# Four edits around the second layer of a two-layer trunk: first weight sections asked for earlier, the z weights split on other engines, one pair without squares, a later row split

## The chip, the cores and the metric

One core of one Trainium2 chip runs the whole kernel. The metric is the device time of one execution in microseconds, as the median of several runs; a profiled execution gives the trace. Engines are called PE (TensorE), DVE (VectorE), ACT (ScalarE), POOL (GpSimd) and SP (SyncE, whose queue issues the transfers).

## The reference

Two layers over x (1024 tokens, 1024 channels), each x <- x + W_out(mixer(RMSNorm(x)) * silu(z)), with z from the same input projection as the mixer's operands; a final RMSNorm follows.

```python
def fox_mixer(h, w_in, b_f, w_out):            # layer 0
    q, k, v, f, z = split(h @ w_in)
    ...                                        # causal attention with a forget gate, 16 heads of 64
    return (o * silu(z)) @ w_out

def nsa_mixer(h, w_in, pe_k, w_ck1, w_ck2, pe_v, w_cv1, w_cv2, w_out):   # layer 1
    q, kc_raw, vc_raw, ks_raw, vs_raw, kw_raw, vw_raw, gate_raw, z = split(h @ w_in)
    kc = compress_blocks(kc_raw, pe_k, w_ck1, w_ck2)
    vc = compress_blocks(vc_raw, pe_v, w_cv1, w_cv2)
    ...                                        # compressed, selected and window attention, three gates
    return (o * silu(z)) @ w_out

def compress_blocks(x, pe, w1, w2):
    ...
    return silu(blk @ w1) @ w2
```

## The kernel before, in words

Every product is taken with operands split into a high and a low part: `mm3` (L224 to L227) issues three matmuls, high by high (L225), high by low (L226), low by high (L227). Layer 0 holds the parts in a 32-bit format, the input projections of layer 1 in F16. An F16 weight is scaled by a power of two first; that scale comes from sums of squares of the weights, which `early.step` gathers during layer 0: each call clears a bias (L181), squares one 128x512 piece on ACT (L182) and then asks for the next piece on SP (L172), with one buffer, so that a piece is asked for when the square before it is done. Calls stand in the K, V, Q and Z sections of the pairs of heads; the V section is `fox_v` (L495), with its two calls at L509, for every pair but pair 0.

**The boundary of the layers.** `out_rest0` (L795) makes the last eight token tiles' results of layer 0 in the order 4, 5, 6, 7, 3, 0, 1, 2: the y matmuls, an add on DVE (L825), squares on ACT, the norm on DVE (L103 to L109, result h_n), then `after0`, which stores the row (L846) and calls `to_hT`: eight transposes on PE (L119, tile pth_n), the high part on ACT (L123), the low part on DVE (L124), into hT, whose half 0 holds tiles 0 to 3 and half 1 tiles 4 to 7. After that `scales`, `section` and `next_w` start layer 1: `next_w` keeps two weight sections ahead, by `load_w16` (L137 to L141, the load of wst) and `split_w16` (L146): high part in one DVE instruction (L147), low part either on DVE in two (L156) or, for kc, v, ka, kr and z, on POOL in eight, four that scale in place (L151) and four that subtract (L152). The first section takes the keys kc0 and kc1 together: half 1 with kc0, half 1 with kc1, then half 0 with each.

**The z weights.** While layer 1's projections and compression run, `load_z` (L901 to L919) brings and splits one of eight z sections at a time: a bias on ACT (zr, L911), then `split_w16` on DVE and POOL, then the next load on SP (zst, L918, one buffer). Nothing uses zw before 970 us. The compression's first product for vc (`cmp_mlp`, hid_vc) takes per step l a load of w_vc (L999), a cast w1h on DVE (L1002), a difference w1l on POOL (L1003), and bh on ACT (L1007) and bl on DVE (L1008), with two buffers for w1h and w1l; between its steps stand sections of q (pn_qr).

**The row split at the end.** `out_start` of layer 1 waits until the first rows of the gated output are stored, loads them (of, L1424), and after `yield 2000` splits them: ohi on ACT (L1429), olo on DVE (L1430). A yield's number is the time that the program gives to other strands of the interleaved code before it takes this one up again. All orders are fixed when the program is built: each engine runs its own list in order.

Of the kernel before, what the change touches and what calls it, by code (L numbers as in the profile page):

```python
# [8 lines left out]
F32 = mybir.dt.float32  # L9
# [4 lines left out]
AF = mybir.ActivationFunctionType  # L14
OP = mybir.AluOpType
# [21 lines left out]
def f(ap):  # L37
    return ap.bitcast(F32)
# [3 lines left out]
def tile_fox_nsa(ctx, tc, a, out):  # L42
# [94 lines left out]
    def load_w16(staged, src, name, scale, gp=False):  # L137


        st = staged.tile([P, KC, P], F32, tag="wst", bufs=1, name=f"wst_{name}")  # L140
        dma(st, src)  # L141
        parts = [wp.tile([P, KC, P], F16, tag=f"w{x}", bufs=2, name=f"w{x}_{name}") for x in ("hi", "lo")]
        return split_w16(st, scale, parts, gp)

    def split_w16(st, scale, parts, gp):
        hi, lo = parts  # L146
        V.tensor_scalar(hi, st, scale, None, OP.mult)  # L147
        if gp:
# [347 lines left out]
    def fox_v(p):  # L496

        w = next_w()
        v = sa.tile([P, 2, 2, 4, P], F16, tag="v", bufs=2, name=f"v_{p}")
        sc = sa.tile([P, 4], F32, tag="vsc", bufs=3, name=f"vsc_{p}")  # L500
        vT = []
        for half in range(2):
            pt = ps_a(f"v{p}_{half}")
            yield from project(w, hT, half, pt)
            vT.append(f(sa.tile([P, 512], F32R, tag="Q", bufs=8, name=f"vT_{p}_{half}")))
            A.activation(vT[half], pt, AF.Abs, accum_out=sc[:, half:half + 1])
            A.copy(vT[half], pt)
            if p:
                early.step(vT[half][:, 0:1])  # L509
        channel_scale(sc, 2, 1 / UP)  # L510
        for half in range(2):
            vs = sa.tile([P, 2, 512], F16, tag="vs", bufs=2, name=f"vs_{p}_{half}")
            A.activation(vs[:, 0], vT[half], AF.Copy, scale=sc[:, 3:4])
            V.scalar_tensor_tensor(vs[:, 1], vT[half], sc[:, 3:4], vs[:, 0], OP.mult, OP.subtract)
            nc.sync.dma_start_transpose(v[:, half].rearrange("p c t d -> p (c t) d"), vs.rearrange("p c t -> p (c t)"))
        ready["v", p] = v, sc[:, 2:3]
# [275 lines left out]
    cols2 = [slice(half * 512, half * 512 + 512) for half in range(2)]  # L792
    gain = []

    def out_rest0(ow, w, after):  # L795

        gB = ow.tile([P, D], F32, name="gB0")
        dma(gB, a["norm_g"][1:2, :].to_broadcast([P, D]))
        gain.extend(gain_scale(gB))
        lh, ll = (ow.tile([P, D], F32R, name=f"o7{x}") for x in "hl")  # L800
        for half in (1, 0):
            dma(f(ll[:, cols2[half]]), oF[7 * P:8 * P, cols2[half]])
        xs0[3] = sk.tile([P, D], F32, tag="KL", name="xr0_3")
        dma(xs0[3], a["x"][3 * P:4 * P, :])
        of, oh, ol = out_tiles("0_3")
        dma(of[:, 0:7, :], oF[0:7 * P, 3 * P:4 * P].rearrange("(k p) t -> p k t", p=P))
        for half in (1, 0):
            A.copy(lh[:, cols2[half]], f(ll[:, cols2[half]]))
            V.tensor_tensor(ll[:, cols2[half]], f(ll[:, cols2[half]]), f(lh[:, cols2[half]]), OP.subtract)
        pend = []  # L810
        for t in (4, 5, 6, 7, 3, 0, 1, 2):
            tk = slice(t * P, (t + 1) * P)
            if t == 3:
                A.copy(oh[:, 0:7, :], of[:, 0:7, :])
                V.tensor_tensor(ol[:, 0:7, :], of[:, 0:7, :], f(oh[:, 0:7, :]), OP.subtract)
# [12 lines left out]
            if len(pend) > 2:
                after(*pend.pop(0))
        for x in pend:  # L830
            after(*x)
# [10 lines left out]
    hT = [[x[:, i] for i in range(2)] for x in hT]  # L842
    ow = tc.alloc_tile_pool(name="ow", bufs=1, reuse_waits="tile")

    def after0(t, xt, h):
        dma(x1[t * P:(t + 1) * P, :], xt)  # L846
        to_hT(h, t, hT, f"n1_{t}")

    out_rest0(ow, ready["wout"], after0)
    W, E = {}, {}  # L850

    def scales(r, kinds, name):


        V.tensor_scalar(r[:, 2], r[:, 1], 2.0 ** 77, None, OP.mult)
        V.tensor_scalar(r[:, 3], r[:, 0], gain[0], 2.0 ** 50, OP.mult, OP.mult)
        for i, x in enumerate(kinds):
            W[x], E[x] = r[:, 2, i:i + 1], r[:, 3, i:i + 1]

    def bound(n, e, sign, name):  # L860

# [5 lines left out]
        return u[:, 0:1], u[:, 1:2]  # L867

    r1 = first[0]
    scales(r1, ("kc", "vc", "q", "z", "g"), "early")  # L870
    rq, eq = bound(r1[:, 1, 2:3], E["q"], -1.0, "q")
    ow.release()
    sk.release()
# [16 lines left out]
    oD = dram.tile([8, 2, P, 512], F32, name="oD")  # L890

    pers = tc.alloc_tile_pool(name="pers", bufs=1, side="right")
    gates = pers.tile([P, NT, 48], F32, name="gates")
    selb = pers.tile([P, GR, 4, 16], F32, name="selb")
    vinv = pers.tile([P, GR], F32, name="vinv")
    pa = tc.alloc_tile_pool(name="pa", bufs=1, reuse_waits="tile")

    nsa_w = [("kc", 0), ("kc", 1), ("qa", 0), ("qa", 1), ("vc", 0), ("vc", 1)]
    nsa_w[4:4] = [("qr", i) for i in range(2)]
    kvo = [("v", 0), ("v", 2), ("v", 1), ("v", 3), ("ka", 0)] + [("kr", i) for i in range(3)]  # L900
    nsa_w += [("qr", i) for i in range(2, 6)] + kvo  # L901
    zt = [h1.tile([P, 4, 2, KC, P], F16, tag=f"h{x}1", name=f"zw{x}") for x in (1, 0)]
    zw = [[zt[p // 4][:, p % 4, x] for x in range(2)] for p in range(8)]

    def load_z(x=None):


        if zload:
            p, st = zload.pop()
            r = pa.tile([P, 1], F32, tag="zr", bufs=2, name=f"zr_{p}")  # L910
            A.activation(r, x, AF.Identity, bias=W["z"], scale=0.0)  # L911
            split_w16(st, r, zw[p], True)
            p += 1
        else:
            p = 0
        if p < 8:
            st = pa.tile([P, KC, P], F32, tag="zst", bufs=1, name=f"zst_{p}")
            dma(st, a["nsa_w"][20 + p])  # L918
            zload.append((p, st))  # L919

    nsa_i = {"kc": 0, "vc": 2, "qa": 4, "qr": 6, "ka": 12, "kr": 13, "v": 16, "z": 20}
    nq, wq = list(nsa_w), []

    def next_w(key):
        while len(wq) < 2 and nq:
            kind, i = nq.pop(0)
            wq.append(((kind, i), load_w16(pers if len(nq) % 2 else wp, a["nsa_w"][nsa_i[kind] + i], f"n{kind}{i}",
                                           W[kind if kind in W else kind[0]], kind in ("kc", "v", "ka", "kr"))))
        k, w = wq.pop(0)
        assert k == key  # L930
        return w

    def section(keys, use):

# [14 lines left out]

    def late_scales():  # L950
        r = roots(sums[:, 41:49], ((0, 4), (4, 8)), "late", pers)
        scales(r, "kv", "late")
        rk, ek = bound(r[:, 1, 0:1], E["k"], 1.0, "k")
        u = pers.tile([P, 4], F32, name="units")
        inverse(u[:, 0:1], rq, rk, SCALE)
        V.tensor_scalar(u[:, 1:2], u[:, 0:1], -1.0, None, OP.mult)
        V.tensor_scalar(u[:, 2:3], E["z"], 0.5, None, OP.mult)
        V.tensor_tensor(u[:, 3:4], E["z"], E["v"], OP.mult)
        ready["units"] = [u[:, i:i + 1] for i in range(4)]
        ready["ek"] = ek  # L960
# [213 lines left out]
    gst = pa.tile([P, KC, 48], F32, name="gst")  # L1174
    dma(gst, a["nsa_w_g"].rearrange("(k p) c -> p k c", p=P))
    gw = pa.tile([P, KC, P], F16, tag="vt", bufs=1, name="gw")
    G.tensor_copy(gw, zero[:, :, None].to_broadcast([P, KC, P]))
    V.tensor_scalar(gw[:, :, 0:48], gst, W["g"], None, OP.mult)
    V.scalar_tensor_tensor(gw[:, :, 64:112], gst, W["g"], gw[:, :, 0:48], OP.mult, OP.subtract)

# [220 lines left out]
    def out_start(rows1):  # L1401
# [29 lines left out]

        yield lambda: met(0)
        load(0)
        yield 2000
        split(0)
        for n, (t, k0, stop) in enumerate(parts):
            if n == 2:
# [338 lines left out]
```

## Time and profile before

| | us |
|---|---|
| median of 3 runs | 1483.13 |
| lowest, highest | 1483.09, 1487.86 |
| profiled execution, its own time | 1481.62 |
| its span | 1479.8 |
| busy PE, DVE, ACT, POOL | 1380.7, 1094.8, 872.1, 600.1 |

The span is the time from the first to the last instruction of the profiled execution. Busy shares are means over stages with different limits, so the places of the edits are read each in its own stretch: its waits on PE, the granted clock there (1.00 is full speed), and the instructions of the other engines in order of time.

### The profile page before, as it was taken

What the parts mean: (1) busy time and instruction counts of PE and PEld (TensorE: products, weight loads), DVE (VectorE), ACT (ScalarE), POOL (GpSimd) and SP (SyncE); (2) the same over time, 40 slices, a digit from 0 to 9 for tenths busy, and PEclk for the clock granted to TensorE, in tenths of its full rate; (3) what the DMA queues carried; (4) which work ended last, traced back from release to release, by engine and by line L of the source; (5) the groups of instructions that cost most, each with busy time, mean ns of one, the idle gap of its engine ahead of it and who ended that gap; (6) DMA issues with size and microseconds to landing.
All of it is one profiled execution on the core that took longest, in us unless ns stands there. A gap on an engine that the chain in (4) does not pass through costs nothing. (4 is left out here: it accounts for less than half of the span.)

```text
span 1479.8 us, 30155 instructions
## 1 busy us (share of the span) xinstructions
PE 1380.7 (93%) x10491; PEld 998.3 (67%) x10491; DVE 1094.8 (74%) x2874; ACT 872.1 (59%) x2190; POOL 600.1 (41%) x816
## 2 busy tenths in 40 slices
PE   5999999999999898989998898889999989999998
PEld 4877888888888767854544444447666766766776
DVE  6586677787877778676754475978988878889844
ACT  5376667676654655345422176657777768787523
POOL 2232323333232320031334665435766657687400
PEclk9999999999999999989998999999999999999999
DMA  7887798988877898454443346646577676677434
GB/s 250 265 177 178 186 196 191 210 180 202 166 162 154 198 214 182 142 172 144 129 125 105 108 128 153 143 128 113 126 153 160 138 165 128 135 157 156 104 136 148
DMA packets 413513, 237.01 MB, mean 160 GB/s; under 512 B 334448, under 2 KB 373040, under 8 KB 413104
## 3 DMA queue, kind: packets, MB, share of 16 engines
q1 hardware_dynamic: 413360, 235.07, 65.9%
q8 instruction: 83, 1.36, 0.4%
q14 instruction: 70, 0.57, 0.1%
HBM read 121.55 MB, written 37.81 MB: 108 GB/s over the span
## 5 line engine op out<-in xcount | busy, mean ns | idle before, releaser
L1532 PE MATMUL S_n<-nk,nq 128*128 128x320 f16 (+5 forms) x768 | 153.3, 314 | 10.1 <-DVE m_n L1540 7.5
L718 ACT ACTIVATE P<-P,m 128x512 f32<-128x512 f32 (+1 forms) x192 | 116.5, 608 | 77.3 <-DVE m L709 76.7
L689 POOL TENSOR_TENSOR Bd<-B,tri 128x128 f32<-128x128 f32 x128 | 62.2, 501 | 240.0 <-DVE m L709 231.3
L1547 POOL TENSOR_TENSOR hl_n<-P_n,hl_n 128x640 f16<-128x640 f32 (+4 forms) x128 | 141.8, 1108 | 9.7
L720 DVE SCALAR_TENSOR_TENSOR hl<-P,hl 128x512 f16<-128x512 f32 (+1 forms) x192 | 116.6, 625 | 21.3 <-ACT hl L719 19.9
L1546 POOL CAST hl_n<-P_n 128x640 f16<-128x640 f32 (+4 forms) x128 | 75.5, 590 | 120.7 <-ACT P_n L1543 98.8
L1543 ACT ACTIVATE P_n<-P_n,m_n,units 128x640 f32<-128x640 f32 (+4 forms) x128 | 100.4, 784 | 34.9 <-DVE m_n L1542 33.8
L1543 ACT ACTIVATE P_n<-P_n,m_n 128x640 f32<-128x640 f32 (+7 forms) x128 | 98.6, 770 | 22.4 <-DVE m_n L1540 21.3
L243 DVE SCALAR_TENSOR_TENSOR ptl_n<-ptp_n,pth_n 128x512 f16<-128x512 f32 (+1 forms) x160 | 99.8, 633 | 10.4 <-ACT pth_n L242 9.4
L1532 PEld LDWEIGHTS <-nq 128*128 128x128 f16 x768 | 70.8, 98 | 53.1 <-issue 16.5
L242 ACT ACTIVATE pth_n<-ptp_n 128x512 f16<-128x512 f32 (+1 forms) x160 | 86.0, 546 | 34.9 <-PE ptp_n L1565 33.0
L225 PE MATMUL y<-wo,ohi 128*128 128x512 f32 x230 | 95.5, 415 | 1.6 <-ACT ohi L602 0.8
L1565 PE MATMUL ptp_n<-ident,P_n 128*128 128x128 f32 x576 | 93.1, 280 | 3.7 <-DVE m_n L1542 1.3
L719 ACT ACTIVATE hl<-P 128x512 f16<-128x512 f32 (+1 forms) x192 | 92.4, 513 | 2.4 <-DMA pT<-hl 1.1
L1540 DVE CUSTOM_DVE_ANT_0 P_n<-S_n,wmask 128x640 f32<-128x640 f32 (+4 forms) x128 | 83.4, 652 | 11.5 <-PE S_n L1532 10.6
L227 PE MATMUL y<-wo,olo 128*128 128x512 f32 x230 | 91.3, 397 | 0.0
L226 PE MATMUL y<-wo,ohi 128*128 128x512 f32 x230 | 90.5, 394 | 0.0
L1565 PEld LDWEIGHTS ptp_n<-ident,P_n 128*128 128x128 f32 x576 | 65.6, 141 | 26.3 <-DVE ptl_n L243 10.7
L1573 PE MATMUL O_n<-nv,pth_n 128*128 128x64 f16 x576 | 71.8, 194 | 4.8 <-ACT pth_n L242 4.6
L1540 DVE CUSTOM_DVE_ANT_0 P_n<-S_n,bias,units 128x640 f32<-128x640 f32 (+1 forms) x64 | 68.9, 1076 | 7.2 <-PE S_n L1532 6.1
L700 PE MATMUL S<-KH,Q 128*128 128x512 f32 (+1 forms) x192 | 64.2, 350 | 9.3 <-DVE m L709 6.5
L1574 PE MATMUL O_n<-nv,pth_n 128*128 128x64 f16 x576 | 71.0, 194 | 0.0
(463 smaller groups left out, 4623.9 us busy)
## 6 DMA issues: line engine op xcount, KB each, us to landing
sq<-in_nsa_w_dram SPq DMA_DIRECT2D x40, 256.0 KB
B<-cD SPq DMA_DIRECT2D x16, 512.0 KB
wo<-wD SPq DMA_DIRECT2D x16, 512.0 KB
nq<-qD SPq DMA_DIRECT2D x64, 128.0 KB
x<-in_x_dram SPq DMA_DIRECT2D x8, 512.0 KB
wst_k<-in_fox_w_dram SPq DMA_DIRECT2D x8, 512.0 KB
wst_v<-in_fox_w_dram SPq DMA_DIRECT2D x8, 512.0 KB
wD<-in_fox_w_out_dram SPq DMA_DIRECT2D x8, 512.0 KB
```

The lines of the kernel that those rows point to most:

```text
L225: T.matmul(ps, wh, mh, start=first, stop=False, **kw)
L226: T.matmul(ps, wh, ml, start=False, stop=False, **kw)
L227: T.matmul(ps, wl, mh, start=False, stop=last, **kw)
L243: V.scalar_tensor_tensor(lo[:, 0:n], pt[:, 0:n], scale, h, OP.mult, OP.subtract)
L718: A.activation(L[:, 0:n], L[:, 0:n], AF.Exp, bias=init, scale=-1.0, accum_out=self.lr[:, col + c:col + c + 1])
L719: A.activation(hi[:, cs], L[:, 0:n], AF.Copy, scale=UP)
L720: V.scalar_tensor_tensor(lo[:, cs], L[:, 0:n], UP, hi[:, cs], OP.mult, OP.subtract)
L1532: T.matmul(ps[:, b, 0:w], self.q[x][:, qi * P:(qi + 1) * P], k[:, k0 + b * w:k0 + b * w + w], start=(x == 0), stop=(x == 1))
L1540: V.tensor_tensor_reduce(dst, src, mk, 1.0 if y else unit, 3e38, OP.add, OP.min, m)
L1543: A.activation(L, L, AF.Exp, bias=m, scale=minus if y else -1.0, accum_out=self.l[:, y, qi:qi + 1])
L1547: G.tensor_tensor(hl[:, n:2 * n], L, hl[:, 0:n], OP.subtract)
L1565: T.transpose(pt[:, (x + i) * P:(x + i + 1) * P], L[:, kb * P - k0:(kb + 1) * P - k0], ident)
```

## The change

1. **Layer boundary.** The scales of the weights are worked out before `out_rest0`, and in its first turn (tile 4) `fill_w` asks for and splits kc0 and kc1. Both come through the pool `wp`; later sections alternate with `pers` as before. A small tile `nil`, made on POOL from a row of tile 2, replaces `zero` as the source from which gw is cleared.
2. **z.** The high part of a z section is made on ACT (one 128x1024 copy with scale), the low part on DVE (two 128x512 instructions); POOL has no part in it.
3. **First pair.** `fox_v` takes squares from pair 2 on, not from pair 1 on; two more squares thus stand at the end of the list.
4. **Row split.** `yield 2000` before the first row split becomes `yield 5000`.

```diff
-            if p:
+            if p > 1:
                 early.step(vT[half][:, 0:1])
...
+    W, E, stage = {}, {}, [wp, wp]
+    def scales(r, kinds):
+        V.tensor_scalar(r[:, 2], r[:, 1], 2.0 ** 77, None, OP.mult)
+        for i, x in enumerate(kinds):
+            W[x] = r[:, 2, i:i + 1]
+    scales(first[0], ("kc", "vc", "q", "z", "g"))
...
+    def fill_w():
+        while len(wq) < 2 and nq:
+            kind, i = nq.pop(0)
+            wq.append(((kind, i), load_w16(stage[len(nq) % 2], a["nsa_w"][nsa_i[kind] + i], f"n{kind}{i}",
+                                           W[kind if kind in W else kind[0]], kind in ("kc", "v", "ka", "kr"))))
...
+            if t == 0:
+                fill_w()
             nm = Norm(ow, xs0[t], f"n0_{t}", 3)
...
     def after0(t, xt, h):
+        if t == 2:
+            G.tensor_scalar(nil, xt[:, 0:1], 0.0, 1.0, OP.mult, OP.mult)
         dma(x1[t * P:(t + 1) * P, :], xt)
...
+    stage[0] = pers
...
-            split_w16(st, r, zw[p], True)
+            hi, lo = zw[p]
+            A.activation(hi, st, AF.Copy, scale=r)
+            for k in range(0, KC, 4):
+                c = slice(k, k + 4)
+                V.scalar_tensor_tensor(lo[:, c], st[:, c], r, hi[:, c], OP.mult, OP.subtract)
...
-    G.tensor_copy(gw, zero[:, :, None].to_broadcast([P, KC, P]))
+    G.tensor_copy(gw, nil[:, :, None].to_broadcast([P, KC, P]))
...
         load(0)
-        yield 2000
+        yield 5000
         split(0)
```

The built program's lists show where the instructions come to stand. At the boundary, PE before (pth_n are the transposes of a tile's normalised row, the first number in the name is the tile):

```order
L119 MATMUL pth_n_0_0_7752<-ident,h_n_0_7665 128x128 x4
L119 MATMUL pth_n_0_1_7759<-ident,h_n_0_7665 128x128 x4
L119 MATMUL pth_n_1_0_7767<-ident,h_n_1_7699 128x128 x4
L119 MATMUL pth_n_1_1_7774<-ident,h_n_1_7699 128x128 x4
L119 MATMUL pth_n_2_0_7782<-ident,h_n_2_7733 128x128 x4
L119 MATMUL pth_n_2_1_7789<-ident,h_n_2_7733 128x128 x4
L225 LDWEIGHTS whi_nkc_7857
L225 MATMUL pn_kc_1_7888<-hT_1_7452,whi_nkc_7857 128x512
```

and after the change:

```order
L119 MATMUL pth_n_0_0_7780<-ident,h_n_0_7693 128x128 x4
L119 MATMUL pth_n_0_1_7787<-ident,h_n_0_7693 128x128 x4
L225 LDWEIGHTS whi_nkc_7668
L225 MATMUL pn_kc_1_7890<-hT_1_7453,whi_nkc_7668 128x512
L226 LDWEIGHTS whi_nkc_7668
L226 MATMUL pn_kc_1_7890<-hT_1_7453,whi_nkc_7668 128x512
L227 LDWEIGHTS wlo_nkc_7669
L227 MATMUL pn_kc_1_7890<-hT_1_7453,wlo_nkc_7669 128x512
```

The 16 transposes of tiles 1 and 2 now stand between the matmuls of kc0, half 1, in four groups after 10, 11, 17 and 18 of them. On DVE the cast whi of kc0 moves ahead of the add of tile 4 and that of kc1 between the two adds of tile 3; on POOL both splits move ahead of the clearing of gw; on SP the load of kc1 moves ahead of the row stores and waits there for POOL's split of kc0, since both use one buffer.

In the vc compression, POOL before (zst and zw are a z section, w1l_vc a step's low part):

```order
L1003 TENSOR_TENSOR w1l_vc_9101<-w_vc_9098,w1h_vc_9100 128x256
L151 TENSOR_SCALAR zst_8894<-zst_8894,zr_9068 128x256 x2
L152 TENSOR_TENSOR zw_7830<-zst_8894,zw_7830 128x256 x2
L151 TENSOR_SCALAR zst_8894<-zst_8894,zr_9068 128x256 x2
L152 TENSOR_TENSOR zw_7830<-zst_8894,zw_7830 128x256 x2
L1003 TENSOR_TENSOR w1l_vc_9126<-w_vc_9123,w1h_vc_9125 128x256
```

and DVE after the change, at the z section ahead of the first steps of vc:

```order
L995 TENSOR_SCALAR raw_vc<-pn_vc_0_8838,roots_early 64x496
L1027 SCALAR_TENSOR_TENSOR bl_vc_8899<-raw_vc,pe,bh_vc_8898 128x252
L942 SCALAR_TENSOR_TENSOR zw_7857<-zst_8734,zr_8867,zw_7857 128x512 x2
L1027 SCALAR_TENSOR_TENSOR bl_vc_8924<-raw_vc,pe,bh_vc_8923 128x252
L1021 CAST w1h_vc_8944<-w_vc_8942 128x256
```

The eight POOL instructions are gone, so the w1l follow one another; the two halves of the low part now stand on DVE between the bl of step 0 and that of step 1, and on ACT the high part between the bh of the same steps.

At the first row split, ACT before (ohi_4_0 is the split row, pth_n here the transposed probabilities of the window attention):

```order
L1543 ACTIVATE P_n_0_1_1_15596,l_n_0_15497<-P_n_0_1_1_15596,m_n_0_1_1_15597,units 128x256
L1543 ACTIVATE P_n_0_0_2_15632,l_n_0_15497<-P_n_0_0_2_15632,m_n_0_0_2_15633 128x384
L1429 CAST ohi_4_0_18300<-of_4_0_18299 128x512
L242 ACTIVATE pth_n_1_3_15591<-ptp_n_1_3_15586 128x512
L1543 ACTIVATE P_n_0_1_2_15660,l_n_0_15497<-P_n_0_1_2_15660,m_n_0_1_2_15661,units 128x384
```

and after the change:

```order
L1562 ACTIVATE P_n_0_1_1_15550,l_n_0_15451<-P_n_0_1_1_15550,m_n_0_1_1_15551,units 128x256
L1562 ACTIVATE P_n_0_0_2_15586,l_n_0_15451<-P_n_0_0_2_15586,m_n_0_0_2_15587 128x384
L1448 CAST ohi_4_0_18254<-of_4_0_18253 128x512
L242 ACTIVATE pth_n_1_3_15545<-ptp_n_1_3_15540 128x512
L1562 ACTIVATE P_n_0_1_2_15614,l_n_0_15451<-P_n_0_1_2_15614,m_n_0_1_2_15615,units 128x384
```

Here nothing moved: the split stands between the same neighbours, and so does olo on DVE and the load on SP.

## Rows read from the trace of the kernel before

**Rows 1.** The page: busy time of each engine over the span, share, instructions.

```profile
PE 1380.7 (93%) x10491; PEld 998.3 (67%) x10491; DVE 1094.8 (74%) x2874; ACT 872.1 (59%) x2190; POOL 600.1 (41%) x816
```

**Rows 2.** What PE waited for over the whole span: line waited at, releaser, total us, times, longest us.

```profile
PE hid_vc L227 <- POOL w1l_vc L1003: 11.7, 3, 4.5
...
PE O_n L1573 <- ACT pth_n L242: 4.6, 3, 4.0
...
PE S L700 <- DVE Q L527: 2.7, 1, 2.7
...
PE kcps L225 <- DVE khh L1018: 1.0, 1, 1.0
```

**Rows 3.** Stretches of the span: busy time and number of instructions of PE, PEld, DVE, ACT, POOL, then the mean granted clock of PE, the DMA share and GB/s.

```profile
135.00:141.00 6.00, 6.00 (x35) 4.78 (x36) 3.68 (x13) 4.71 (x13) 0.88 (x2) 0.72 0.58 162
...
642.00:655.00 13.00, 6.72 (x35) 4.90 (x33) 12.53 (x25) 7.52 (x19) 1.86 (x3) 0.73 0.70 239
655.00:662.00 7.00, 6.62 (x25) 2.60 (x25) 2.77 (x7) 0.60 (x3) 7.00 (x12) 0.77 0.87 272
...
776.00:790.00 14.00, 10.14 (x48) 5.53 (x46) 6.36 (x12) 3.77 (x6) 7.31 (x11) 0.88 0.33 95
790.00:815.00 25.00, 21.03 (x106) 12.48 (x105) 12.68 (x27) 7.48 (x12) 10.34 (x16) 0.86 0.36 107
815.00:850.00 35.00, 30.54 (x151) 16.96 (x149) 17.14 (x36) 5.32 (x10) 23.39 (x39) 0.90 0.35 102
...
1204.00:1212.00 8.00, 5.67 (x61) 4.21 (x62) 4.75 (x12) 4.65 (x11) 3.26 (x4) 0.57 1.00 159
```

**Rows 4.** PE at the boundary in order of time: start us, us, instruction, idle before it and releaser.

```profile
646.33 0.66 PE L119 MATMUL pth_n<-ident,h_n 128*128 128x128 f32 x4 [0.62 <-DVE hT L124]
650.02 1.97 PE L119 MATMUL pth_n<-ident,h_n 128*128 128x128 f32 x8 [3.04 <-DVE hT L124]
...
654.37 0.63 PE L225 MATMUL pn_kc<-hT,whi_nkc 128*128 128x512 f16 x1
...
658.26 0.38 PE L227 MATMUL pn_kc<-hT,wlo_nkc 128*128 128x512 f16 x1
658.47 0.38 PE L225 MATMUL pn_kc<-hT,whi_nkc 128*128 128x512 f16 x1
```

**Rows 5.** DVE at the boundary, same columns.

```profile
636.14 0.69 DVE L825 TENSOR_TENSOR xr<-y,xr 128x512 f32<-128x512 f32 x1 [3.27 <-PE y L227]
...
639.15 1.41 DVE L109 SCALAR_TENSOR_TENSOR h_n<-xr,st_n,gB 128x512 f32<-128x512 f32 x2
...
653.26 0.74 DVE L147 TENSOR_SCALAR whi_nkc<-wst_nkc,roots_early 128x1024 f16<-128x1024 f32 x1
...
655.84 1.09 DVE L147 TENSOR_SCALAR whi_nkc<-wst_nkc,roots_early 128x1024 f16<-128x1024 f32 x1
```

**Rows 6.** POOL around the boundary, same columns: idle until the clearing of gw, then the split of kc0 begins.

```profile
647.05 1.04 POOL L1177 CAST gw<-zero 128x1024 f16<-128x1024 f32 x1 [73.50 <-PE pth_n L119]
654.18 0.94 POOL L151 TENSOR_SCALAR wst_nkc<-wst_nkc,roots_early 128x256 f32<-128x256 f32 x2 [6.09 <-issue]
...
656.36 1.77 POOL L151 TENSOR_SCALAR wst_nkc<-wst_nkc,roots_early 128x256 f32<-128x256 f32 x2
```

**Rows 7.** POOL's instructions on a z section's staging tile: line, engine, operation, count, duration in ns (least, median, most), first and last start.

```profile
L151 POOL TENSOR_SCALAR zst<-zst,zr x32: 474/482/2031, 729.1 to 854.3; 128x256 f32<-128x256 f32 x32
L152 POOL TENSOR_TENSOR zw<-zst,zw x32: 662/669/910, 732.0 to 855.4; 128x256 f16<-128x256 f32 x32
```

**Rows 8.** POOL in the vc compression, in order of time: the z splits and the w1l behind them.

```profile
774.15 1.41 POOL L151 TENSOR_SCALAR zst<-zst,zr 128x256 f32<-128x256 f32 x2 [17.82 <-DVE zw L147]
...
779.71 1.41 POOL L1003 TENSOR_TENSOR w1l_vc<-w_vc,w1h_vc 128x256 fp32r<-128x256 f32 x2
...
798.90 1.41 POOL L1003 TENSOR_TENSOR w1l_vc<-w_vc,w1h_vc 128x256 fp32r<-128x256 f32 x2
```

**Rows 9.** PE at the three waits, in order of time.

```profile
780.48 0.39 PE L227 MATMUL hid_vc<-bh_vc,w1l_vc 128*128 128x252 f32 x1 [3.28 <-POOL w1l_vc L1003]
...
799.68 0.58 PE L227 MATMUL hid_vc<-bh_vc,w1l_vc 128*128 128x252 f32 x1 [3.97 <-POOL w1l_vc L1003]
...
823.15 0.58 PE L227 MATMUL hid_vc<-bh_vc,w1l_vc 128*128 128x252 f32 x1 [4.46 <-POOL w1l_vc L1003]
```

**Rows 10.** DVE and ACT where z sections stand: a low part on DVE of the same shape as the new one, the bias and the bh on ACT, a square of 128x1024 on ACT, DVE's idle time behind a z section.

```profile
754.32 0.74 DVE L974 TENSOR_SCALAR raw_vc<-pn_vc,roots_early 64x512 f32<-64x512 f32 x1 [2.52 <-ACT raw_vc L972]
759.42 0.75 DVE L156 SCALAR_TENSOR_TENSOR wlo_nqr<-wst_nqr,roots_early,whi_nqr 128x512 f16<-128x512 f32 x1
...
773.71 1.40 ACT L1007 ACTIVATE bh_vc<-raw_vc,pe 128x252 fp32r<-128x252 f32 x2
...
724.98 1.16 ACT L182 ACTIVATE sq<-sq,zg 128x1024 f32<-128x1024 f32 x1
```

**Rows 11.** The first pair in layer 0: ACT's squares and what they waited for, and the load of the second on SP.

```profile
117.79 0.72 ACT L182 ACTIVATE sq<-sq,zg 128x512 f32<-128x512 f32 x1 [1.65 <-DMA sq<-in_nsa_w_dram]
...
132.77 0.72 ACT L182 ACTIVATE sq<-sq,zg 128x512 f32<-128x512 f32 x1 [2.20 <-DMA sq<-in_nsa_w_dram]
...
128.71 0.53 SPq L172 DMA_DIRECT2D sq<-in_nsa_w_dram  x1
```

**Rows 12.** The first row split: ACT waits for the row's load.

```profile
1205.16 0.62 ACT L1429 CAST ohi<-of 128x512 fp32r<-128x512 f32 x1 [4.18 <-DMA of<-oF]
```

More of the change, by code (lines that the diff above doesn't have):

```diff
@@ L793, in tile_fox_nsa, with next_w @@
     gain = []
+    W, E, stage = {}, {}, [wp, wp]
[4 more added lines that the diff above has]
+    scales(first[0], ("kc", "vc", "q", "z", "g"))
+    nsa_w = [("kc", 0), ("kc", 1), ("qa", 0), ("qa", 1), ("vc", 0), ("vc", 1)]
+    nsa_w[4:4] = [("qr", i) for i in range(2)]
+    kvo = [("v", 0), ("v", 2), ("v", 1), ("v", 3), ("ka", 0)] + [("kr", i) for i in range(3)]
+    nsa_w += [("qr", i) for i in range(2, 6)] + kvo
+    nsa_i = {"kc": 0, "vc": 2, "qa": 4, "qr": 6, "ka": 12, "kr": 13, "v": 16, "z": 20}
+    nq, wq = list(nsa_w), []
+    def fill_w():
[3 more added lines that the diff above has]
+                                           W[kind if kind in W else kind[0]], kind in ("kc", "v", "ka", "kr"))))
+    def next_w(key):
+        fill_w()
+        k, w = wq.pop(0)
+        assert k == key
+        return w
     def out_rest0(ow, w, after):
@@ L815, in out_rest0 @@
                 V.tensor_tensor(ol[:, 0:7, :], of[:, 0:7, :], f(oh[:, 0:7, :]), OP.subtract)
+            if t == 0:
+                fill_w()
             nm = Norm(ow, xs0[t], f"n0_{t}", 3)
@@ L843, in tile_fox_nsa @@
     ow = tc.alloc_tile_pool(name="ow", bufs=1, reuse_waits="tile")
+    nil = h1.tile([P, 1], F32, name="nil")
     def after0(t, xt, h):
+        if t == 2:
+            G.tensor_scalar(nil, xt[:, 0:1], 0.0, 1.0, OP.mult, OP.mult)
         dma(x1[t * P:(t + 1) * P, :], xt)
@@ L849, in tile_fox_nsa, with undo @@
     out_rest0(ow, ready["wout"], after0)
-    W, E = {}, {}
-    def scales(r, kinds, name):
-        V.tensor_scalar(r[:, 2], r[:, 1], 2.0 ** 77, None, OP.mult)
+    def undo(r, kinds):
         V.tensor_scalar(r[:, 3], r[:, 0], gain[0], 2.0 ** 50, OP.mult, OP.mult)
         for i, x in enumerate(kinds):
-            W[x], E[x] = r[:, 2, i:i + 1], r[:, 3, i:i + 1]
+            E[x] = r[:, 3, i:i + 1]
     def bound(n, e, sign, name):
@@ L869, in tile_fox_nsa @@
     r1 = first[0]
-    scales(r1, ("kc", "vc", "q", "z", "g"), "early")
+    undo(r1, ("kc", "vc", "q", "z", "g"))
     rq, eq = bound(r1[:, 1, 2:3], E["q"], -1.0, "q")
@@ L896, in tile_fox_nsa @@
     pa = tc.alloc_tile_pool(name="pa", bufs=1, reuse_waits="tile")
[L898 to L901, printed above, removed]
     zt = [h1.tile([P, 4, 2, KC, P], F16, tag=f"h{x}1", name=f"zw{x}") for x in (1, 0)]
@@ L919, in load_z @@
             zload.append((p, st))
[L921 to L931, printed above, removed]
     def section(keys, use):
@@ L951, in late_scales @@
         r = roots(sums[:, 41:49], ((0, 4), (4, 8)), "late", pers)
-        scales(r, "kv", "late")
+        scales(r, "kv")
+        undo(r, "kv")
         rk, ek = bound(r[:, 1, 0:1], E["k"], 1.0, "k")
```

## The prediction

> **What bounds the kernel now.** I read the busy shares first: PE works 93% of the span [rows 1], so time can come off only where PE stands idle or runs at half clock. The list of PE's waits comes next [rows 2]: the wait for w1l_vc is 11.7 us in three pieces, the one for Q of the first pair 2.7, the one for pth_n at the row split 4.0 at its longest. Then the stretches with their granted clock [rows 3]. PE's matmuls show two speeds only, 0.43 us apart at the start of pn_kc and 0.21 after 658.26 [rows 4], so a mean clock below 1.00 gives the time at half clock as 2 x (1 - clock) x length: 135 to 141 holds 3.4 us of it, 642 to 662 10.2 (7.0 and 3.2), 776 to 790 3.4, 790 to 815 7.0, 815 to 850 7.0, 1204 to 1212 6.9. Each lies behind a wait of PE, and while PE has work, half of it is lost. So a wait that goes can be worth its length and up to half of the slow time behind it. Last I read each place in order of time on the engine that releases PE.
>
> **The layer boundary.** Before, PE does the transposes of tiles 1 and 2 as their rows become ready, waits 3.04 us ahead of tile 1's, and starts pn_kc at 654.37 [rows 4]. DVE is the cause: it works 12.53 of the 13 us from 642 [rows 3]. POOL has been idle for 73.50 us at 647.05 and does kc0's split from 654.18 [rows 6]. After, kc0 and kc1 are split long before, and pn_kc follows tile 0's transposes, since half 1 of hT (tiles 4 to 7) is ready. Those transposes end at about 647.0 (646.33 + 0.66) [rows 4]. The two casts of kc, 0.74 and up to 1.09 [rows 5], go from behind the chain to places ahead of it. The first falls before the 3.27 us for which DVE waits on y [rows 5] and is swallowed there; the second lies behind it and delays what follows by 0.74, and by about 0.4 more if POOL's split of kc1 stretches DVE (1.09 against 0.74, with POOL busy [rows 5, 6]). So pn_kc starts at about 648.2, 6.2 us earlier. Against that, the 16 transposes now stand among its matmuls. Eight took 1.97 us at half clock [rows 4], so 16 cost 2.0 at full clock and 3.9 at half. Half 0, which needs tiles 1 and 2, comes only after 48 matmuls, kc0 and kc1 of half 1 (10 us at 0.21), later than the last hT. If the clock comes back 3.9 us after the start, as it did before (654.37 to 658.26 [rows 4]), the loss to half clock is the same and the gain is 6.2 - 2.1 = 4.1. If it stays at half to 658.26, 5 us are lost in place of 1.9 and the transposes cost 2 more: about 1.1. With no half clock behind the start, 6. I take **4.1 (1 to 6)**, since PE's work there is as dense as what brought the clock back before. SP: kc1's load shares a buffer with kc0 and holds the row stores behind it until POOL has split kc0, some 5 us; nobody reads those stores before the end stage, so nothing. The nil tile is one small POOL instruction in an idle engine: nothing.
>
> **z.** POOL's price per section is 4 x 0.482 + 4 x 0.669 = 4.6 us, and the worst ones took 2.03 for one [rows 7]. Three of the eight stand right ahead of a w1l for which PE waits: POOL starts one at 774.15 and reaches w1l at 779.71, and the next at 798.90 [rows 8]; PE resumes at 780.48, 799.68 and 823.15, after 3.28, 3.97 and 4.46 [rows 9]. After, each section costs ACT 1.16 (an activation of 128x1024) and DVE 2 x 0.75 in place of 0.74 [rows 10]. What is late next is bl and w1h, which stand on DVE behind the low part. At the first wait: bh of step 0 ends at about 774.4 [rows 10], the high part at 775.5, the low part at 777.0, bl of step 1 at 777.8, w1h and w1l of step 2 (0.7 each) at 779.1; so PE resumes 1.4 earlier, 1.5 with the clock's small change. At the second, where high and low parts stand a whole q section ahead of the steps, about 0.5 of wait stays, a gain of 3.5. At the third the fills of the vc operand (three or four of 0.6 on POOL) stay ahead, 1.7 of wait, a gain of 2.8. Sum 7.8 of 11.7. Slow time: 17.4 us behind the three, worth 8.7; I keep nearly all of the first (0.5 gained of 1.7), gain all of the second (3.4 of 3.5) and 2.4 of the third: 6.3. Together **14.1 (4 to 20.4)**, the ends being a return of most waits (below) and all of 11.7 + 8.7. Earlier, at kcps, PE waits 1.0 for DVE's khh [rows 2] behind a z section; DVE is dense there, and the added 0.75 lengthens the wait: **-0.75 (0 to -1.5)**. The other four sections lie where DVE waits afterwards, 2.52 us at 754.32 [rows 10], or after the last hid_vc: nothing; were that slack gone, 4 x 0.75 = 3.
>
> The trace shows a wait of 2.7 us followed by half clock from 135 to 141 [rows 2, 3]; so a wait of 1.8 that stays at the first section may still cost clock, as I count it. [...]
>
> **The first pair.** ACT waits 1.65 and 2.20 for pieces to square [rows 11], the second because its load stands on SP at 128.71 behind transfers, and PE then waits 2.7 for Q [rows 2], followed by 3.4 us at half clock. After, the V section is without both squares, so Q's first square finds its piece loaded long ago, and Q's halves come 1.4 to 3.4 us earlier; but the next load is then late in the same way, and ACT holds its exponentials until about the same time as before. I take **2.0 (0 to 4.4**, 4.4 being the wait and half of 3.4). The two squares moved to the end of the list fall into ACT's slack in layer 0 (59% busy [rows 1]); without it they cost 2 x 0.72 and the bias, 2.
>
> **The row split.** ACT waits 4.18 us for the row [rows 12], and PE 4.0 behind it [rows 2]. The order of ACT and DVE at that place is the same after the change, so the wait stays: **0 (-2 to 2)**; only some matmuls of y move.
>
> **The sum.** 4.1 + 14.1 - 0.75 + 2.0 + 0 = 19.45 off the profiled execution's 1481.62: 1462.2. The median of before lies 1.5 above that execution, so the forecast is **1463.7 us**.
>
> **Rivals.** *The z waits come back on ACT and DVE.* These lists are in order, and the low part waits for ACT's high part; any bl, w1h or w1l behind it waits too. Then of 11.7 us only 4 go and the clock still drops: 4.1 + 4 - 0.75 + 2 = 9.35, 1473.8 us. For it: the low part at the first section stands between two bl. Against it: 1.16 + 1.50 is less than POOL's 4.6 to 5.6, and q sections lie between. POOL's instructions do stretch beside DVE's, 0.94 for two against 1.77 [rows 6]; a w1l behind a low part would meet this, 0.75 a time. [...] Chance 0.18.
>
> *The row split does work.* With some y matmuls behind, PE has other work while ACT waits, or the load comes earlier beside what stands behind it. Then 4.0 and half of 6.9 come on top, 7.4: 1456.3 us. For it: matmuls of y move to behind the last heads on PE. Against it: what PE waits for is ACT, whose list has not changed there. Chance 0.14. That this edit does nothing at its wait, and so isn't what it says, is in the forecast.
>
> *Slower: the z sections become serial.* If each of the eight held the chain of PE for all of its 1.16 + 1.50 = 2.66 us, and the three old waits stayed because w1h stands behind, it would be 8 x 2.66 = 21.3 against 6.1 from the boundary and the first pair: 15.2 slower, 1498.3 us. It passes 0.5% (7.4 us) from (6.1 + 7.4) / 8 = 1.7 a section. Against it: DVE waits after several of the sections [rows 10], and the old waits cannot stay whole when POOL's 4.6 are gone. Chance 0.04.
>
> **The numbers.** The forecast has 0.64, the rivals 0.18, 0.14 and 0.04. 0.5%, 7.4 us, is about what can be told from no change, so faster is under 1475.7. The first rival straddles that, so some 0.08 of it goes to no change, with 0.01 from the forecast's lower end: faster 0.87, same 0.09, slower 0.04. The range, 1453 to 1475.5, takes in the row split's case and the z waits that come back; it leaves out the ends at which all the unknown costs go one way.
>
> **What would show it.** Right: pn_kc starts 5 to 6 us earlier against the end of the y matmuls; PE's wait for w1l_vc is under 5 us in all and 790 to 815 shows a clock near 1.00; the wait for Q in the first pair is shorter; PE's 4.0 at the row split and ACT's 4.18 are still there. Wrong: a new wait of hid_vc for bl, w1h or zw's neighbours of over 8 us, half clock unchanged in the vc compression, or a boundary where PE still waits for hT ahead of pn_kc.

## The result: 1.5% faster, and the profile after

The change took **1461.06 us** in the median of 6 runs (1459.80 to 1463.23) against 1483.59 of the kernel before beside it; the ratio is 0.9848, 95% interval [0.9828, 0.9869], so 22.5 us less. The forecast was 1463.7 within 1453 to 1475.5. The profiled execution took 1463.23 us, its span 1461.4.

What PE waits for now, in the view of [rows 2] (line, releaser, total us, times, longest us):

```profile
PE O_n L1592 <- ACT pth_n L242: 3.9, 2, 3.5
...
PE S_n L1551 <- DMA nq<-qD: 3.8, 2, 3.6
...
PE hid_vc L226 <- DVE bl_vc L1027: 1.3, 2, 1.0
...
PE kcps L226 <- DVE khl L1038: 0.9, 1, 0.9
...
PE kcps L225 <- DVE khh L1037: 0.7, 1, 0.7
...
PE hid_vc L227 <- POOL w1l_vc L1022: 0.2, 1, 0.2
```

The wait for w1l_vc, 11.7 us in [rows 2], is 0.2; 1.3 for bl_vc stand in its place. The first pair's wait for Q is no longer in the list. The wait for ACT at the row split is still there with 3.5 (4.0 before), and so is ACT's own wait for the row ahead of it, against [rows 12]:

```profile
1178.95 0.62 ACT L1448 CAST ohi<-of 128x512 fp32r<-128x512 f32 x1 [3.69 <-DMA of<-oF]
```

The stretches that answer to [rows 3], each moved by what the program had gained up to it (columns as there; the last but two is the granted clock):

```profile
130.00:136.00 6.00, 6.00 (x42) 4.77 (x41) 4.09 (x12) 4.43 (x12) 3.72 (x6) 1.00 0.58 133
640.00:653.00 13.00, 10.10 (x52) 5.71 (x51) 12.29 (x25) 7.57 (x19) 3.79 (x5) 0.87 0.71 237
653.00:660.00 7.00, 7.00 (x34) 3.23 (x33) 3.35 (x8) 3.91 (x8) 1.41 (x2) 1.00 1.06 345
768.00:782.00 14.00, 13.20 (x68) 8.36 (x68) 9.32 (x18) 5.07 (x8) 4.18 (x5) 0.88 0.39 106
782.00:795.00 13.00, 13.00 (x76) 8.08 (x75) 8.54 (x16) 6.66 (x10) 4.83 (x6) 1.00 0.56 171
795.00:827.00 32.00, 31.25 (x174) 17.88 (x173) 21.60 (x47) 9.67 (x16) 16.39 (x25) 1.00 0.47 144
1178.00:1186.00 8.00, 5.88 (x55) 4.39 (x56) 4.56 (x11) 4.35 (x10) 2.90 (x4) 0.57 0.83 175
```

Half clock, as 2 x (1 - clock) x length: none in the first pair (3.4 before), 3.4 at the boundary (10.2), 3.4 in the vc compression (17.4), and unchanged at the row split, 6.9 (6.9). Over all thirteen profiles of this case the first pair has none with edit 3 and 3.4 without it, and the boundary 3.4 or none with edit 1 and 10.2 or 13.7 without it. In the vc compression the profile of the change is the only one of nine with edit 2 that has any. At the row split the 6.9 does not belong to the kernel: the second profile of the change has 3.4.

PE at the boundary, against [rows 4]:

```profile
642.86 0.93 PE L119 MATMUL pth_n<-ident,h_n 128*128 128x128 f32 x4 [2.02 <-DVE h_n L109]
644.10 1.12 PE L119 MATMUL pth_n<-ident,h_n 128*128 128x128 f32 x4 [0.31 <-DVE hT L124]
645.01 0.63 PE L225 MATMUL pn_kc<-hT,whi_nkc 128*128 128x512 f16 x1
...
646.59 0.38 PE L226 MATMUL pn_kc<-hT,whi_nkc 128*128 128x512 f16 x1
...
648.62 0.55 PE L119 MATMUL pth_n<-ident,h_n 128*128 128x128 f32 x3 [0.58 <-DVE hT L124]
```

pn_kc follows tile 0's transposes directly; a transpose of tile 1 waits 0.58 among its matmuls, where [rows 4] show 3.04. The clock is back 1.6 us after the first matmul of pn_kc, not 3.9.

The staging tile of z, against [rows 7]:

```profile
L942 DVE SCALAR_TENSOR_TENSOR zw<-zst,zr,zw x16: 740/752/1152, 720.1 to 826.5; 128x512 f16<-128x512 f32 x16
...
L939 ACT ACTIVATE zw<-zst,zr x8: 1135/1149/1150, 718.0 to 824.6; 128x1024 f16<-128x1024 f32 x8
```

**Where the time went.** I took the same PE matmul in two traces and subtracted its start times; I call the difference the shift. The table gives what each kernel's trace is ahead (-) or behind (+) of the kernel before at nine places: the q of the first pair, the z section behind it, the first product with the last pair's rows in layer 0, the first hid_kc, the first hid_vc, vcps at the end of the vc compression, the first O_n of the window attention, an O_n 55 us after the row split, and the last y. Each is one profiled execution.

| kernel | 121 | 144 | 617 | 682 | 774 | 840 | 1001 | 1261 | 1472 |
|---|---|---|---|---|---|---|---|---|---|
| the change | -0.6 | -5.2 | -3.1 | -8.1 | -8.1 | -23.5 | -25.4 | -25.5 | -18.5 |
| the change, second | -0.2 | -4.7 | -1.9 | -6.0 | -4.9 | -21.8 | -22.8 | -24.3 | -17.9 |
| without edit 4, first | -0.6 | -5.1 | -5.0 | -9.6 | -8.8 | -25.8 | -26.9 | -28.1 | -24.5 |
| without edit 4, second | -0.5 | -5.1 | -4.7 | -9.2 | -11.7 | -28.7 | -30.8 | -32.1 | -30.1 |
| without edit 4, third | 0.0 | -4.6 | -1.7 | -5.8 | -4.6 | -21.5 | -23.3 | -25.3 | -19.2 |
| edit 1 alone | +0.8 | +1.3 | +1.2 | -3.3 | -2.5 | -2.2 | -1.0 | -1.8 | +0.6 |
| edit 2 alone | -0.4 | -0.8 | +0.9 | +0.5 | +1.2 | -15.7 | -16.1 | -17.5 | -17.3 |
| edit 3 alone | +0.2 | -4.3 | -3.6 | -3.1 | -3.0 | -3.0 | -4.9 | -5.5 | -2.4 |
| edit 4 alone | -0.6 | -0.7 | +0.7 | +0.3 | +1.1 | +1.9 | +0.7 | -0.6 | +0.9 |

So the change gains 4.6 us in the first pair, 5.0 at the boundary and 15.4 in the vc compression, and gives back 2.1 between 144 and 617 and 7.0 after 1261. Over the kernels of the table the first pair gives 4.5 or 4.6 where edit 3 is in, the boundary 4.1 to 5.0 where edit 1 is in, and the vc compression 16.9 or 17.0 where edit 2 is in, but for the 15.4 of the change itself. Outside the places of the edits, traces differ by one to three us a stage even for one and the same kernel, in part by where half clock falls: between the first hid_kc and the first hid_vc the three traces without edit 4 hold 6.8 us of it, none and 10.2 (the kernel before 6.8).

### The profile page after: what moved, and what is told of

It reads as the page before. It is cut to its first block, busy times and chain, and to the rows that moved or that the text cites. A ratio compares the mean times of both kernels' runs of the same rounds, so it can differ in the third digit from the quotient of the medians.

```text
span 1461.4 us, 30097 instructions
## 1 busy us (share of the span) xinstructions
PE 1376.6 (94%) x10491; PEld 997.5 (68%) x10491; DVE 1096.5 (75%) x2882; ACT 880.7 (60%) x2198; POOL 562.1 (38%) x753
## 4 chain that ended last, share of the span: by engine, by line
PE 31%; DVE 11%; ACT 5%; issue 3%; DMA 2%; POOL 2%; SPq 1%; DVEq 0%; ACTq 0%; POOLq 0%
PE S_n L1551 5%; PE ptp_n L1584 3%; DVE P_n L1559 2%; ACT P_n L1562 2%; PE y L225 2%; PE y L226 2%; PE y L227 2%; PE O_n L1592 1%; PE O_n L1594 1%; ACT cP L1277 1%; PE O_n L1593 1%; DVE ptl_n L243 1%; PE nz L227 1%; PE nz L226 1%; PE nz L225 1%
```

## Experiments

**Each edit alone, and the change without the fourth.** Edit 4 taken back is

```diff
-        yield 5000
+        yield 2000
         split(0)
```

> The change without its fourth edit (yield 2000 kept). In the profile of the change, 25.4 us are gained at 1290 us and only 18.9 at the end. Theory A: the fourth edit costs this, as it moves y matmuls out of the last heads; then this kernel is 4 to 7 us faster than the change (1454 to 1457 us), its shift against before stays at about -25 to the end. Theory B: the last heads lose it because everything before them is earlier (a late q load, 3.6 us, and a clock drop); then it is within 1.5 us of the change's 1461, and the q wait is still there. In both the 3.5 us wait for ACT at the row split stays.

1458.58 us in the median (1457.19 to 1460.06), ratio 0.9842 [0.9816, 0.9868]: 2.5 below the change, with intervals that overlap. PE's wait for ACT at the row split stayed, 3.1 at its longest. The shift went from -28.1 to -24.5 after 1261, where the change went from -25.5 to -18.5. That pointed to theory A, but not clearly; see the repetition below.

Edit 2 alone:

```diff
-            split_w16(st, r, zw[p], True)
+            hi, lo = zw[p]
+            A.activation(hi, st, AF.Copy, scale=r)
+            for k in range(0, KC, 4):
+                c = slice(k, k + 4)
+                V.scalar_tensor_tensor(lo[:, c], st[:, c], r, hi[:, c], OP.mult, OP.subtract)
```

> The kernel before with the second edit alone (z split on ACT and DVE). Theory A (the forecast's step): 14 us off, 1466 to 1471 us, the three waits for w1l_vc gone and the clock full from 780 to 830. Rival: the waits come back on bl or w1h and the clock still drops: 4 us off, 1479.

1463.97 us, ratio 0.9881 [0.9855, 0.9907]: 18.7 off, more than theory A's number and far from the rival's. PE's waits between 600 and 850 us there:

```profile
PE hid_vc L226 <- DVE bl_vc L1012: 1.3, 2, 1.0
...
PE kcps L226 <- DVE khl L1023: 0.9, 1, 0.9
PE kcps L225 <- DVE khh L1022: 0.7, 1, 0.7
...
PE hid_vc L227 <- POOL w1l_vc L1007: 0.2, 1, 0.2
```

and its stretches in the vc compression, with the stretch at kcps first:

```profile
728.00:742.00 14.00, 12.39 (x53) 5.46 (x51) 10.43 (x19) 3.44 (x9) 0.78 (x1) 0.88 0.49 147
775.00:789.00 14.00, 12.46 (x70) 8.12 (x71) 10.68 (x19) 7.16 (x11) 4.36 (x5) 1.00 0.40 133
789.00:814.00 25.00, 24.27 (x136) 14.72 (x134) 18.93 (x43) 10.31 (x15) 11.54 (x14) 1.00 0.51 155
```

The three waits are gone, and the clock is full where [rows 3] have 0.88 and 0.86. In this trace the shift goes from +1.2 to -15.7 between the first hid_vc and vcps, 16.9 us. At kcps PE waits 1.6, hardly more than before, but half clock falls there. It does so with the old z split too, in the traces of edit 1 alone and of edit 4 alone, so nothing shows that this edit brings it.

Edit 1 alone (fill_w in the first turn of out_rest0, nil, scales moved ahead; the other edits taken back):

> The kernel before with the first edit alone (kc0 and kc1 asked for ahead). Theory A: 4 to 6 us off (1477.5 to 1479.5), all of it between the last y matmuls of layer 0 and kc, and the shift kept afterwards. Rival: the later stages give it back (waits at the vc stage grow by what was gained): within 1.5 us of before.

1480.07 us in 12 runs, ratio 0.9981 [0.9963, 1.0]: 2.6 off, between the two theories, with an interval that reaches 1.00. The trace shows 4.5 us gained between 617 and 682 (+1.2 to -3.3), as theory A says. Of that, 2.3 is gone again by the first O_n and 1.6 more by the end. Later stages gave most of it back in this execution; whether they do so in all of them one profile can't tell.

Edit 3 alone:

```diff
-            if p:
+            if p > 1:
```

> The kernel before with the third edit alone (no squares in pair 1's V section). The change's trace shows 4.5 us gained at 137 us and 2.1 lost between 575 and 595 us. Theory A: both belong to this edit, 2 to 2.5 us off at 620 us, since the two squares at the end of the list delay the last pairs. Theory B: the loss at 575 is a clock drop that comes with any shift or none; then 3.5 to 5 us are off.

1478.22 us in 12 runs, ratio 0.9973 [0.9952, 0.9993]: 4.4 off. The trace gains 4.5 at the first pair and keeps it to 617 within 0.7. So the 2.1 that the change lost between 575 and 595 need not come from the two squares at the end of the list: theory B. What falls there is a piece of half clock, 3.4 us from 578.2 in the change. The traces of edit 2 alone and of edit 4 alone, whose lists of squares are the old ones, have it too (from 582.0 and 581.7), and this trace has none. Of the three traces without edit 4 the first has none either and loses 0.1 between 144 and 617; the third has it and loses 2.9. ACT in the first pair of the change, against [rows 11]:

```profile
127.39 0.72 ACT L182 ACTIVATE sq<-sq,zg 128x512 f32<-128x512 f32 x1
...
132.91 0.73 ACT L182 ACTIVATE sq<-sq,zg 128x512 f32<-128x512 f32 x1
...
133.75 0.73 ACT L718 ACTIVATE P<-P,m 128x512 f32<-128x512 f32 x1
```

and SP's loads there:

```profile
126.21 3.50 SPq L515 DMA_TRANSPOSE v<-vs  x2
129.81 0.53 SPq L172 DMA_DIRECT2D sq<-in_nsa_w_dram  x1
```

Neither square of Q waits. The load of the second is issued at 129.81, 3.1 us ahead of its use.

**The fourth edit: repeated, alone, and done in another way.** The change, and the change without its fourth edit, once more on one chip, and edit 4 alone:

> The change once more, beside the kernel without its fourth edit, since one profile of each differs by 6 us and the medians by 2.5. Theory A (the fourth edit costs time in the last heads): 2 to 4 us slower than the kernel without it, with the late q load (over 3 us of wait) near 1318 us again. Theory B (chance): within 1 us of it, and the wait is not there again.

> The change without its fourth edit once more, on the same chip. Theory A: 1457 to 1459 us, the wait for q in the last heads again near 1.3 us. Theory B: equal to the change within 1 us.

> The kernel before with the fourth edit alone. Forecast: no change, the wait of PE for ACT at the row split (4.0 us) stays. Theory A (it costs time in the last heads): 2 to 4 us slower than before, all lost after 1300 us. Theory B: within 1.5 us of before.

The change: 1461.45 us, ratio 0.9848 [0.9824, 0.9872]. Without edit 4: 1458.68, 0.9824 [0.9802, 0.9845]. Edit 4 alone: 1484.68 against 1484.17, ratio 1.0013 [0.9996, 1.003], which is theory B. Alone, the four edits thus give 2.6, 18.7, 4.4 and -0.5 in the medians, 25.2 in all; together they give 22.5. The late q load came back in the second profile of the change (3.19 us of wait, 3.56 in the first):

```profile
1318.00 1.46 PE L1551 MATMUL S_n<-nk,nq 128*128 128x320 f16 x4 [3.19 <-DMA nq<-qD]
```

and without edit 4 it was shorter:

```profile
1309.48 0.31 PE L1551 MATMUL S_n<-nk,nq 128*128 128x320 f16 x1 [1.31 <-DMA nq<-qD]
```

Edit 4 alone showed 2.1 us of it, no more than the kernel before (2.1 in two waits). Three times without edit 4 the median was below the change's two, by 1.5 to 2.9 us. But the third profile without it (below) also lost 6.1 us after 1261, and all intervals overlap. Half clock takes part in these losses: in the last heads the change has 3.4 us of it and its second profile 6.8, the first and the third without edit 4 have 3.4, and the second, which lost least (2.0), has none. So edit 4 saves nothing and may cost 1 to 3 us; that is as far as this goes.

Then the split was moved by what a yield can't do. The first split's scale is a column of ones worked out from the newest transposed probabilities:

```diff
         load(0)
-        yield 5000
-        split(0)
+        yield 2000
+        one = consts.tile([P, 1], F32, name="one_row")
+        V.tensor_scalar(one, ready["pth"][:, 0:1], 0.0, 1.0, OP.mult, OP.add)
+        of, oh, ol = (x[:, 0:4, :] for x in pend[0])
+        A.activation(oh, of, AF.Copy, scale=one)
+        V.tensor_tensor(ol, of, f(oh), OP.subtract)
```

with `ready["pth"] = hi` in `split_t`, so that the split depends on the probabilities that stand ahead of it in the program. On ACT it then stands some 150 instructions later, at 1308 us in the trace where it stood at 1180.

> The change without its fourth edit, and the first row split tied to a later instruction: its scale is a column of ones worked out from the newest transposed probabilities (one small DVE instruction added), so that the split stands some 150 instructions later on ACT, right ahead of the matmuls that use it. Theory A (ACT waited for the row's load in its list, and PE behind it; a yield can't move that, a dependence can): PE's wait for ACT near 1177 us goes, with the half clock behind it: 3.5 to 7 us faster than without this (1452 to 1455). Rival: PE is no faster, since another wait (the heads' DVE or a DMA) takes its place: within 1.5 us.

> The same with yield 600 in place of 2000 ahead of the split, so that y matmuls stand more evenly among the last heads. Theory A (the fourth edit cost time because y matmuls, the last heads' filler, came later): as fast as the one with 2000 or 1 to 2 us faster. Theory B (the place of y there does not matter): equal within 1 us.

> The change without its fourth edit, beside these two on one chip: 1457 to 1460, with PE's wait for ACT of 3 to 3.6 us near 1177 us.

With the dependence 1456.77 us (1455.51 to 1462.88), ratio 0.9838 [0.9812, 0.9864]; with yield 600 as well **1455.59** (1452.79 to 1456.41), 0.9822 [0.9796, 0.9848], the lowest median of all kernels here; without either 1459.52, 0.9846 [0.9818, 0.9874]. The three intervals overlap, and the second run without edit 4, on another chip, has 0.9824 with neither. The stretches around the row split, first without (third run) and then with the dependence:

```profile
1170.00:1190.00 20.00, 17.00 (x222) 12.31 (x221) 13.60 (x41) 12.95 (x33) 11.52 (x16) 1.00 0.78 206
```

```profile
1170.00:1190.00 20.00, 20.00 (x258) 14.54 (x257) 16.74 (x51) 15.07 (x38) 12.43 (x17) 1.00 0.82 193
```

PE is busy all of the time in place of 17.00 of 20. The clock is full in both: this execution without the dependence is the one of three in which no half clock follows the wait (the other two have 3.4 us of it each, the change 6.9). PE's wait for ACT, 3.0 in the third run without, is gone from the list, and two waits of 0.4 and 0.3 behind it. The two traces part by 4.4 us between 1173 and 1201 (from -1.0 to -5.3). So the wait and what it cost in this stretch are shown to go. The whole is 2.8 to 3.9 in the medians, in the direction of theory A and below or at the lower end of its 3.5 to 7, and not clear of noise. Theory B on the yield of 600 can't be told from A: 1.2 us lie between the two.

**Both parts of z on DVE:**

```diff
-            hi, lo = zw[p]
-            A.activation(hi, st, AF.Copy, scale=r)
-            ...
+            split_w16(st, r, zw[p], False)
```

> Edits one to three, but both parts of z on DVE (0.74 + 2 x 0.75) and none on ACT. Theory A (POOL's place ahead of w1l was the whole cause, any other engine will do): within 1.5 us of the kernel without the fourth edit. Theory B (DVE is dense in the vc compression, the share taken by ACT matters): 2 to 5 us slower than it, with new waits for bl, w1h or khh.

1461.57 us (1459.34 to 1464.26), ratio 0.9848 [0.9826, 0.9870], against 1458.68 with ACT's share: 2.9 slower. PE's waits between 600 and 830 us:

```profile
PE kcps L225 <- DVE khh L1033: 1.9, 1, 1.9
PE hid_vc L225 <- DVE w1h_vc L1017: 1.0, 1, 1.0
PE hid_vc L227 <- POOL w1l_vc L1018: 0.9, 2, 0.8
PE hid_vc L226 <- DVE bl_vc L1023: 0.9, 1, 0.9
```

PE waits 4.7 us for khh, w1h, w1l and bl; with ACT's share it was 0.7, 0.3, 0.2 and 1.3, 2.5 in all (khl the other way, 0.4 against 0.9). Theory B by the medians, though the intervals overlap, and the trace places only part of the 2.9: it gains 15.8 us between the first hid_vc and vcps, where those with ACT's share and no edit 4 gain 16.9 or 17.0. POOL's place ahead of w1l was most of the cause, since another engine there brings most of the gain; that the share for ACT is worth the rest is likely, not shown.

## Why the prediction was right, point by point

**The boundary: right.** 4.1 was forecast, 5.0 measured in the change and 4.5 with edit 1 alone. pn_kc was forecast at 648.2 on the old time; it came at 645.01, which is 648.1 with the 3.1 us gained by then. DVE did stretch beside POOL's split as I allowed for: h_n took 1.99 for two where [rows 5] have 1.41. What I had left as a bound, that the clock comes back sooner, made the rest: 1.6 us after the first matmul of pn_kc in place of 3.9. That dense work of PE brings it back was my estimate of the cause; no run shows it.

**z: the mechanism was right, the size too small.** The rival in which ACT and DVE take POOL's place is out: 1.3 us for bl_vc are left, not 7.7. 14.1 was forecast inside the compression; 15.4 was measured in the change and 16.9 with edit 2 alone. The terms that were mis-sized are the waits that I let stay, 0.5 at the second section and 1.7 at the third, and with them the clock: the 1.3 that is left stands at the first section. The half clock that I kept there, 3.4 us, did come in the change, but in none of the eight other profiles with edit 2, so that this term fitted was luck; half of it, 1.7, is about what parts 15.4 from 16.9. I had priced w1h at 0.7, as it took next to POOL's z split (0.71); in the change it took 0.28 at that section. DVE before, then after, both at the first section:

```profile
775.87 0.71 DVE L1002 CAST w1h_vc<-w_vc 128x256 fp32r<-128x256 f32 x1
```

```profile
766.77 1.42 DVE L942 SCALAR_TENSOR_TENSOR zw<-zst,zr,zw 128x512 f16<-128x512 f32 x2 [0.39 <-ACT zw L939]
768.10 0.64 DVE L1027 SCALAR_TENSOR_TENSOR bl_vc<-raw_vc,pe,bh_vc 128x252 fp32r<-128x252 f32 x1
768.67 0.28 DVE L1021 CAST w1h_vc<-w_vc 128x256 fp32r<-128x256 f32 x1
```

So POOL's split stood in PE's way at two points, of very different size. By its place it cost the wait for w1l: this cast had ended at 776.58, and POOL came to w1l at 779.71 [rows 8], so a shorter cast would not have helped there. The cast itself took 0.71 beside it, and PE waited 0.58 us for its result, up to 776.73; in the change this section has no wait for w1h. That 0.43 of the 0.58 came from the longer cast is an estimate, 0.71 against 0.28. In the trace of before, casts of w_vc beside POOL's z instructions took anything from 0.28 to 0.71, and seven that ran while POOL was idle 0.29 each. At kcps I had forecast 0.75 lost; PE's waits there are 1.6 against 1.5 before, so nearly nothing. Half clock falls behind them in nine of the thirteen profiles, two with the old z split among them, and not in those of the kernel before and of the change.

**The first pair: right in direction, the step on ACT failed.** 2.0 was forecast, 4.6 and 4.5 measured, just over my upper bound of 4.4. The failing step was "the next load is then late in the same way, and ACT holds its exponentials until about the same time". The load is not late, since it is issued right behind the transposes at 129.81, with its use at 132.91; ACT reaches the exponentials at 133.75, where it reached them at 137.42 before. The load has that time because ACT, no longer held by the first square, now waits for PE ahead of Q's second half:

```profile
129.98 0.59 ACT L526 ACTIVATE Q<-q 64x512 fp32r<-64x512 f32 x1 [1.78 <-PE q L227]
```

All of PE's 2.7 and all of the half clock went.

**The row split: right.** Zero was forecast; the wait stayed (3.5, and 2.9 in the second profile) and half clock too (6.9 and 3.4). The order of the lists told it: PE waits for ACT, and ACT's list had not changed at that place. The experiment with a dependence shows the price of that wait, 4.4 us in one pair of executions without half clock there; with it, the rival's 4.0 and half of 6.9 would be 7.4.

**What was in no term** is the loss after 1261 us, 7.0 in the profile of the change, where I had written only that some matmuls of y move. It is not all the fourth edit's, since kernels without it lose 2.0 to 6.1 there too. What of it is chance is open. Together these misses nearly cancel: 4.1 + 14.1 - 0.75 + 2.0 against 5.0 + 15.4 + 0 + 4.6, 25.0 in place of 19.45; of it 2.1 and 7.0 are given back, and 2.6 come from small shifts elsewhere, which makes the 18.5 of the profiled execution. The medians lie further apart, 22.5. That the forecast of 1463.7 came within 2.6 us of the result is thus in part luck.

**The clock.** I had counted a wait of 1.8 us as one that may still cost clock, going by the 2.7 ahead of the half clock in the first pair. The trace with edit 2 alone shows half clock behind less: in the 3.4 us from 732.0 PE was busy 1.79, and in the next 3.4 the clock was 0.52.

```profile
732.00:735.40 3.40, 1.79 (x10) 1.15 (x10) 2.45 (x6) 0.42 (x1) 0.78 (x1) 1.00 0.83 297
735.40:738.80 3.40, 3.40 (x10) 1.16 (x8) 1.22 (x4) 0.70 (x3) 0.00 (x0) 0.52 0.32 111
```

PE's stalls of 1.6 us in two pieces were followed by half clock here; half of the 3.4 us, 1.7, is an estimate of what they can cost beside. They are not always: the change has the same stalls there, 0.9 and 0.7 us, and no half clock behind them. In the traces of the kernel before and of the change half clock comes, up to PE's last matmul, in pieces of 3.41, 6.83 and 10.24 us, that is one, two or three steps of 3.413, and within each trace their starts lie whole steps apart: in the kernel before, 135.93 to 139.34 and 781.04 to 784.45 are wholly at half clock, and their starts are 645.11 us, or 189 steps of 3.413, apart.

```profile
135.93:139.34 3.41, 3.41 (x9) 2.65 (x9) 2.25 (x10) 2.85 (x10) 0.88 (x2) 0.50 0.57 182
781.04:784.45 3.41, 3.41 (x10) 1.22 (x9) 1.72 (x3) 1.41 (x2) 0.81 (x2) 0.50 0.79 254
```

The same wait fell on such steps in two ways. The wait for ACT at the row split was 3.1 us in the first trace without edit 4 and 3.0 in the third. In the first nearly all of it fell into one step, and half clock followed; in the third it was shared by two steps, and none followed. First trace, then third:

```profile
1175.73:1179.14 3.41, 0.63 (x5) 0.27 (x5) 1.15 (x2) 1.80 (x5) 2.12 (x3) 1.00 0.82 195
1179.14:1182.55 3.41, 3.41 (x29) 2.62 (x28) 2.71 (x7) 1.86 (x5) 1.41 (x2) 0.50 0.78 230
```

```profile
1176.90:1180.31 3.41, 1.65 (x20) 1.27 (x18) 0.91 (x4) 0.33 (x2) 1.48 (x3) 1.00 1.00 261
1180.31:1183.73 3.42, 2.17 (x23) 1.22 (x24) 2.56 (x5) 2.88 (x7) 2.21 (x3) 1.00 0.61 150
```

PE's busy share alone does not settle it, since 1.79 us was followed by half clock above and 1.65 was not here; what else counts is open.

## What to carry to other kernels

Work that nothing needs for 150 us can still be on the critical path, when it stands in an engine's list ahead of something small that is needed at once (here 11.7 us of PE's waits for w1l); look at who is queued behind it, not at who reads it. Before believing that an edit moves an instruction, read the engine's list: a hint in program order did nothing at the place it was aimed at, while a data dependence moved the instruction (from 1180 to 1308 us) and removed the wait of 3.0 us. Where an edit takes an engine away from a place, price the neighbours by what they take without it, not by their durations beside it (the cast w1h: 0.28 us and 0.71).

## What was not expected of the hardware

A cast of 128x256 on DVE took 0.28 us alone and up to 0.71 beside POOL's split. The granted clock fell to half after a stretch of 3.4 us with PE 1.79 us busy, and in another trace stayed full after one with 1.65. A wait of nearly the same length at the row split was followed by half clock in one execution (3.1 us, the first without edit 4) and by none in another (3.0, the third). Traces of one kernel part by some 3 us within a stage although their lists are the same: between the first hid_kc and the first hid_vc the three traces without edit 4 moved by +0.8, -2.5 and +1.2 against the kernel before.
